# Second layer's experts in whole float32: two products in column halves, eleven more weight places

## The chip, the core and the metric

One Trainium2 chip, one core of it. The metric is the time on the device in microseconds, the median over runs; lower is better. A core has TensorE (PE), VectorE (DVE), ScalarE (ACT), GpSimd (POOL), SyncE (SP, which here only issues transfers) and 16 DMA engines.

## What is computed

Two layers. In each, four token mixers (retention, neighbourhood attention, an S5 scan, windowed attention) work on 512 tokens of width 1024 beside 256 context tokens, and behind them comes a mixture of 32 experts with a two-step router. The second layer runs its experts for the 512 tokens alone. The part that matters here, of the reference:

```python
def hier_moe(xf, rw1, rb1, rw2, rb2, w1, w3, w2):
    ...
    top_v, top_i = lax.top_k(lg2, TOP_K)
    gate = p_grp * jax.nn.softmax(top_v, axis=-1)
    ...
    def expert_block(args):
        xblk, e = args
        hid = jax.nn.silu(xblk @ w1[e]) * (xblk @ w3[e])
        return hid @ w2[e]

    yb = lax.map(expert_block, (xb, blk_expert)).reshape(cap, d)
    y = jax.ops.segment_sum(yb * buf_gate[:, None].astype(yb.dtype), buf_tok, num_segments=n + 1)
```

All is float32. w1 and w3 of an expert are 1024 x 512, w2 is 512 x 1024: three times 2 MB, so 32 experts of a layer read 201 MB.

## The kernel before

*Weights.* A `Stream` (lines 133 to 205) brings weights through fixed places of 512 KB in SBUF, 128 partitions of 2 x 512 float32. `want` (line 156) notes which slice comes next; `load` (line 171) issues a transfer on SP's queue (line 175) whenever a place is free; `feed` (line 178) takes the oldest landed place and splits it into a pair of tiles in the format fp32r, and the place is free again. The split (line 434) is a copy to the high part on ScalarE (line 436) and a subtraction for the low part on VectorE (line 437). There are five pairs, in an arena of their own (`parts`, which the profile calls big_r). `take` hands landed pairs to a product and `release` gives them back.

*A product* (line 553) makes three passes over TensorE for each slice of 128 rows, high by high, high by low and low by high, on lines 560 to 562, into PSUM.

*An expert.* Tokens of an expert are gathered from DRAM by an indirect transfer on GpSimd's queue (line 1894) into 56 rows in the second layer (72 in the first). `turn_x` and `turned` transpose them on TensorE (line 1827), four transposes to a call, and split the result into high and low. `hidden` (line 1839) runs `product` for exp_w1, then for exp_w3, each with eight slices; between the two it transposes the hidden rows of the expert before and the tokens of the next. SiLU is on ScalarE (line 1851), the product of the two halves on VectorE (line 1852). `out_rows` (line 1856) multiplies by exp_w2 on lines 1865 to 1867, 24 passes into two PSUM tiles, and VectorE scales the rows by gate and modulation (line 1874). A scatter that adds (line 1897, GpSimd's queue) puts them into the output rows in DRAM; each waits for the one before.

*Order.* `moe` (line 1890) runs hidden(e), then the output of e-1, for 32 experts; the weights are wanted in the same order, exp_w1 whole, exp_w3 whole, then exp_w2 of the expert before. `moe_open` (line 1876) takes the tiles of the stage and adds places, which come free as the mixers' and the router's tiles end. Before the experts, `moe` feeds four places with GpSimd as the engine of the subtraction (line 1922) and six with VectorE (line 1926), beside the routing. A loop over tokens beyond the 56 rows (line 1977) follows; with this input it runs no turn.

A scheduler of the language settles the order of instructions on each engine from the program and its tiles; the order on SP's queue follows the order of `want`.

## Time and profile before

| What | Value |
|---|---|
| time, median of 3 runs | 2857.58 us (2855.39 to 2862.84) |
| the profiled execution's own time | 2857.83 us |
| its span, first to last instruction | 2856.0 us |
| mean granted TensorE clock | 0.97 |
| busy share of the span: PE, DVE, ACT, POOL | 93%, 73%, 51%, 23% |
| moved by DMA in the whole span | 699.37 MB, 245 GB/s |

The span is cut by the page into 40 slices of 71.4 us. The second layer's experts fill the slices from the 32nd on (2237 us), the first layer's from about the 14th to the 21st. Busy shares are over the whole span, so a stage has to be read by its own stretch. Weights that wait in places, and the places that wait for a split, do not show as busy time anywhere; they show as waits of SP's queue, in front of line 175. The tiles have names: raw and big hold places and other float32 data, big_r the split pairs, sc the PSUM tiles of `hidden`, mm those of `out_rows`, tr those of transposes, mod those of the modulation product (line 482).

### The profile page before, as it was taken

The page shows a single profiled execution, that of the slowest core. Times are in us where ns is not written, and L with a number is a line of the kernel's source. Part 1 is how long each engine was busy: PE and PEld are TensorE (multiplying, and loading weights), DVE is VectorE, ACT ScalarE, POOL GpSimd, SP SyncE. Part 2 cuts the span into 40 slices and gives each one's busy share as a digit, 9 for nine tenths or more (in the row PEclk, how much of TensorE's full clock was granted, in tenths as well). Part 3 has the DMA queues.
Part 4 walks back from the last instruction along what each step waited for, and adds up shares of the span by engine and source line. Part 5 has one row for each costly group of instructions (what it writes and reads, how often), then busy time and mean ns, then how long its engine had stood idle before and what let it go on. Part 6 is the DMA issues. An engine that isn't in the chain of part 4 may idle for free. (4 is left out here: it accounts for less than half of the span.)

```text
span 2856.0 us, 39093 instructions
## 1 busy us (share of the span) xinstructions
PE 2662.6 (93%) x13190; PEld 1808.5 (63%) x13190; DVE 2077.0 (73%) x3921; ACT 1463.3 (51%) x2219; POOL 659.4 (23%) x596
## 2 busy tenths in 40 slices
PE   5999999999998899999996799999999799999997
PEld 2777767777786556665553477777887455555443
DVE  6754455656347989998886668746846999998887
ACT  3322343532232678887775334533324577776665
POOL 2231211011013621111112311021101533323432
PEclk8999999999999899999998999999999799999999
DMA  8687545244427899999997765465435899999994
GB/s 280 198 266 221 153 133 185 81 151 154 159 96 256 287 342 376 359 354 356 372 374 234 230 178 166 125 208 168 137 109 192 275 369 376 372 358 335 343 348 119
DMA packets 268646, 699.37 MB, mean 245 GB/s; under 512 B 64836, under 2 KB 83512, under 8 KB 268440
## 3 DMA queue, kind: packets, MB, share of 16 engines
q1 hardware_dynamic: 170672, 531.30, 51.9%
q0 software_dynamic: 39744, 113.86, 14.9%
q10 hardware_dynamic: 58024, 51.65, 5.8%
q8 instruction: 106, 1.74, 0.2%
q14 instruction: 100, 0.82, 0.1%
HBM read 622.48 MB, written 80.44 MB: 246 GB/s over the span
## 5 line engine op out<-in xcount | busy, mean ns | idle before, releaser
L437 DVE TENSOR_TENSOR big_r<-big,big_r 128x1024 fp32r<-128x1024 f32 x512 | 613.8, 1223 | 80.1 <-ACT big_r L436 76.3
L436 ACT CAST big_r<-big 128x1024 fp32r<-128x1024 f32 x517 | 532.9, 1052 | 146.9 <-PE mm L562 74.9
L560 PE MATMUL mm<-big_r,turned 128*128 128x512 f32 x1248 | 515.7, 414 | 13.4 <-ACT turned L436 7.0
L561 PE MATMUL mm<-big_r,turned 128*128 128x512 f32 x1248 | 506.7, 406 | 3.8 <-DVE big_r L437 3.8
L562 PE MATMUL mm<-big_r,turned 128*128 128x512 f32 x1248 | 506.3, 406 | 0.3 <-DVE turned L437 0.3
L437 DVE TENSOR_TENSOR big_r<-raw,big_r 128x1024 fp32r<-128x1024 f32 x392 | 464.1, 1218 | 41.5 <-ACT big_r L436 35.4
L436 ACT CAST big_r<-raw 128x1024 fp32r<-128x1024 f32 x395 | 403.6, 1051 | 65.8 <-PE sc L562 32.8
L561 PE MATMUL sc<-big_r 128*72 128x512 f32 (+1 forms) x1024 | 409.7, 400 | 19.5 <-DVE big_r L437 18.4
L560 PE MATMUL sc<-big_r 128*72 128x512 f32 (+1 forms) x1024 | 407.3, 398 | 0.0
L562 PE MATMUL sc<-big_r 128*72 128x512 f32 (+1 forms) x1024 | 405.1, 396 | 0.0
L560 PEld LDWEIGHTS mm<-big_r,turned 128*128 128x128 f32 x1248 | 238.3, 191 | 96.2 <-issue 28.7
L562 PEld LDWEIGHTS mm<-big_r,turned 128*128 128x128 f32 x1248 | 238.0, 191 | 57.7 <-issue 6.5
L561 PEld LDWEIGHTS mm<-big_r,turned 128*128 128x128 f32 x1248 | 238.7, 191 | 55.8 <-issue 5.1
L561 PEld LDWEIGHTS sc<-big_r 128*72 128x72 f32 (+1 forms) x1024 | 138.4, 135 | 139.0 <-DVE big_r L437 55.0
L1897 POOL DMA_INDIRECT out_dram<-big x32 | 159.5, 4984 | 264.6 <-DVE big L1874 260.2
L1866 PE MATMUL mm<-big_r 128*72 128x512 f32 (+1 forms) x512 | 204.0, 398 | 0.4
L560 PEld LDWEIGHTS sc<-big_r 128*72 128x72 f32 (+1 forms) x1024 | 139.1, 136 | 100.6 <-ACT big_r L436 7.7
L1867 PE MATMUL mm<-big_r 128*72 128x512 f32 (+1 forms) x512 | 201.3, 393 | 0.0
L562 PEld LDWEIGHTS sc<-big_r 128*72 128x72 f32 (+1 forms) x1024 | 138.8, 136 | 85.9 <-issue 1.2
L1865 PE MATMUL mm<-big_r 128*72 128x512 f32 (+1 forms) x512 | 184.5, 394 | 1.1 <-DVE big L1874 0.6
L1382 ACT ACTIVATE wa<-mm 128x512 f32<-128x512 f32 x80 | 47.7, 596 | 230.2 <-PE mm L562 229.9
L1368 DVE SCALAR_TENSOR_TENSOR wa<-wa,mm 128x512 f32<-128x512 f32 x60 | 41.1, 686 | 138.6 <-PE mm L562 132.6
(381 smaller groups left out, 3764.5 us busy)
## 6 DMA issues: line engine op xcount, KB each, us to landing
big<-in_exp_w_dram SPq DMA_DIRECT2D x393, 512.0 KB
raw<-in_exp_w_dram SPq DMA_DIRECT2D x375, 512.0 KB
big<-in_mod_w_dram SPq DMA_DIRECT2D x96, 512.0 KB
big<-in_w_in_dram SPq DMA_DIRECT2D x68, 512.0 KB
big<-in_w_in_dram SPq DMA_DIRECT2D x48, 256.0 KB
big<-s_wc POOLq DMA_DIRECT2D x16, 576.0 KB, 5.6
big<-s_ph POOLq DMA_DIRECT2D x16, 388.0 KB, 3.9
big<-s_wb POOLq DMA_DIRECT2D x16, 384.0 KB, 4.1
```

The lines of the kernel that those rows point to most:

```text
L436: return (self.nc.scalar.copy(hi, src), (v or self.nc.vector).tensor_tensor(lo, src, hi.bitcast(F32), op=OP.subtract))
L437: (v or self.nc.vector).tensor_tensor(lo, src, hi.bitcast(F32), op=OP.subtract))
L560: nc.tensor.matmul(ps, ah, wh, start=(k == 0), stop=False)
L561: nc.tensor.matmul(ps, ah, wl, start=False, stop=False)
L562: nc.tensor.matmul(ps, al, wh, start=False, stop=(k == n - 1))
L1368: nc.vector.scalar_tensor_tensor(tg, tg, 1.0, pb, op0=OP.add, op1=OP.mult)
L1382: nc.scalar.activation(tg, pg, AF.Tanh, scale=0.5)
L1865: nc.tensor.matmul(o, hh.v[:, k, :n], w[:, 0, half], start=(k == 0), stop=False)
L1866: nc.tensor.matmul(o, hh.v[:, k, :n], w[:, 1, half], start=False, stop=False)
L1867: nc.tensor.matmul(o, hl.v[:, k, :n], w[:, 0, half], start=False, stop=(k == 3))
L1897: scatter = lambda y, i: nc.gpsimd.indirect_dma_start(out=ya, out_offset=bass.IndirectOffsetOnAxis(ap=i, axis=0), in_=y, in_offset=None, b ...
```

## The change

In the second layer the weights are used as they land, in float32, and are not split. `want` marks such a slice as whole, `feed` leaves it alone, and `take_whole` hands the places themselves to the products; a place goes back to the stream when both products of its slice are issued. A float32 product is one instruction for a slice in place of three. `hidden_whole` writes the product with exp_w1 to PSUM partitions 64 to 119 and the one with exp_w3 to partitions 0 to 55 of one tile, slice by slice in turn, and `want_hidden` orders exp_w1 and exp_w3 in turn to suit. `out_whole` does the same with the two column halves of exp_w2. The transposed tokens and hidden rows are copied once (ScalarE or VectorE) in place of a split. The gate is copied to partitions 64 and up, where the second half's rows lie.

`moe_open` gives the arena of the pairs up in the second layer, opens a float32 arena of the same size instead, named whole, and lays eleven places and the transposed tiles into it. These places are added behind all others. The feeds beside the routing fall away in the second layer. The first layer stays as it is.

The diff, without the loop that runs no turn:

```diff
--- before.py
+++ after.py
         for b in stages:
             self.stages.remove(b)
-    def want(self, pieces):
-
-        self.todo.append(pieces)
+    def want(self, pieces, whole=False):
+
+        self.todo.append((pieces, whole))
         self.load()
     def want_cols(self, src, pieces, nk):
...
     def load(self):
         while self.todo and self.stages and not self.pause:
             b = self.stages.pop(0)
-            for dst, src in self.todo.pop(0):
+            pieces, whole = self.todo.pop(0)
+            for dst, src in pieces:
                 self.prog.nc.sync.dma_start(dst(b.v), src)
-            self.staged.append(b)
+            self.staged.append((b, whole))
     def feed(self, v=None):
-        if self.staged and self.pairs:
-            b, s = self.staged.pop(0), self.pairs.pop(0)
+        if self.staged and self.pairs and not self.staged[0][1]:
+            b, s = self.staged.pop(0)[0], self.pairs.pop(0)
             with self.prog.after(*self.behind):
                 self.prog.split(s.v[:, 0], s.v[:, 1], b.v, v)
             self.ready.append(s)
-            if b in self.once:
-                self.once.remove(b)
-            else:
-                self.stages.append(b)
-            self.load()
+            self.back(b)
             return True
+
+    def back(self, b):
+
+        if b in self.once:
+            self.once.remove(b)
+        else:
+            self.stages.append(b)
+        self.load()
+
+    def take_whole(self, n):
+
+        out, self.staged = self.staged[:n], self.staged[n:]
+        assert len(out) == n and all(w for _, w in out) and not (self.ready or self.live)
+        return [b for b, _ in out]
+
     def take(self, n):
...
         bigs = pool("bigs", 1)
         n_r, n = 13312, 18784
-        self.parts = Arena(bigs.tile([128, n_r], F32R, name="big_r"), n_r)
+        self.parts_pool = tc.alloc_tile_pool(name="parts", bufs=1, side="left")
+        ctx.callback(lambda: self.parts_pool.release())
+        self.parts = Arena(self.parts_pool.tile([128, n_r], F32R, name="big_r"), n_r)
         self.arena = Arena(bigs.tile([128, n], F32, name="big"), n)
...
+
+    def open_whole(self):
+
+        self.parts_pool.release()
+        self.parts_pool = self.tc.alloc_tile_pool(name="whole", bufs=1, side="left")
+        n = 13312
+        self.parts = Arena(self.parts_pool.tile([128, n], F32, name="whole"), n)
+        self.s.pairs = []
     def rbuf(self, *shape):
...
     def want_hidden(self, s, l, e):
-        for name in ("exp_w1", "exp_w3"):
-            src = self.rows_at(name, l, e).rearrange("(p k) c -> p k c", k=8)
+        srcs = [self.rows_at(name, l, e).rearrange("(p k) c -> p k c", k=8) for name in ("exp_w1", "exp_w3")]
+        if l:
             for k in range(0, 8, 2):
-                s.want([(lambda st: st, src[:, k : k + 2])])
+                for src in srcs:
+                    s.want([(lambda st: st, src[:, k : k + 2])], True)
+        else:
+            for src in srcs:
+                for k in range(0, 8, 2):
+                    s.want([(lambda st: st, src[:, k : k + 2])])
     def want_out(self, s, l, e):
         src = self.rows_at("exp_w2", l, e).rearrange("(p k) c -> p k c", k=4)
         for k in range(4):
-            s.want([(lambda st: st.rearrange("p h c -> p (h c)"), src[:, k])])
+            s.want([(lambda st: st.rearrange("p h c -> p (h c)"), src[:, k])], bool(l))
     def rows_at(self, name, l, e):
         w = self.A[name]
...
-        self.split(hi.v[:, ks, :n], lo.v[:, ks, :n], tr[:, :, :n])
+        if lo is None:
+            (nc.vector.tensor_copy if q else nc.scalar.copy)(hi.v[:, ks, :n], tr[:, :, :n])
+        else:
+            self.split(hi.v[:, ks, :n], lo.v[:, ks, :n], tr[:, :, :n])
     def turn_x(self, n, x, b=None):
...
         nc.vector.tensor_tensor(hid[:n].rearrange("p (k c) -> p c k", k=4), t.rearrange("p (c k) -> p c k", k=4),
                                 hp[1][:n].rearrange("p (c k) -> p c k", k=4), op=OP.mult)
         return hid
+
+    def hidden_whole(self, n, xT, between):
+
+
+        nc = self.nc
+        x = xT[0].v
+        two = n <= 64
+        ps = [self.ps_sc.tile([128, 512], F32, name="sc") for _ in range(1 if two else 2)]
+
+        o = [ps[0][64 : 64 + n], ps[0][:n]] if two else [ps[0][:n], ps[1][:n]]
+        for j in range(4):
+            ws = self.s.take_whole(2)
+            for k in (2 * j, 2 * j + 1):
+                for m in range(2):
+                    nc.tensor.matmul(o[m], x[:, k, :n], ws[m].v[:, k % 2], start=(k == 0), stop=(k == 7))
+            for w in ws:
+                self.s.back(w)
+            if j == 1:
+                between()
+        hid = self.hid.v
+        t = self.wa()[:n]
+        nc.scalar.activation(t, o[0], AF.Silu)
+        nc.vector.tensor_tensor(hid[:n].rearrange("p (k c) -> p c k", k=4), t.rearrange("p (c k) -> p c k", k=4),
+                                o[1].rearrange("p (c k) -> p c k", k=4), op=OP.mult)
+        return hid
+
+    def out_whole(self, n, y, hT, gate, by):
+
+        nc = self.nc
+        h = hT[0].v
+        two = n <= 64
+        ws = self.s.take_whole(4)
+        ps = [self.ps_mm.tile([128, 512], F32, name="mm") for _ in range(1 if two else 2)]
+        at = [0, 64 if two else 0]
+        o = [ps[0][:n], ps[-1][at[1] : at[1] + n]]
+        for k, w in enumerate(ws):
+            for half in range(2):
+                nc.tensor.matmul(o[half], h[:, k, :n], w.v[:, half], start=(k == 0), stop=(k == 3))
+            self.s.back(w)
+        for half in range(2):
+            c = slice(half * 512, half * 512 + 512)
+            nc.vector.scalar_tensor_tensor(y[:n, c], o[half], gate(at[half]), by[at[half] : at[half] + n, c],
+                                           op0=OP.mult, op1=OP.mult)
+        self.copied = None
     def out_rows(self, n, y, hT, gate, by):
...
                 nc.vector.scalar_tensor_tensor(y[:n, c], ps[half][:n], gate, by[:n, c], op0=OP.mult, op1=OP.mult)
     def moe_open(self, l, C):
-        self.xT = [(self.rbuf(128, 8, C), self.rbuf(128, 8, C)) for _ in range(2)]
-        self.hT = self.rbuf(128, 4, C), self.rbuf(128, 4, C)
+        if l:
+            self.open_whole()
+
+            room = self.rbuf(128, 12, 128)
+            extra = [self.rbuf(128, 2, 512) for _ in range(11)]
+            room.free()
+            self.xT = [(self.rbuf(128, 8, C), None) for _ in range(2)]
+            self.hT = self.rbuf(128, 4, C), None
+        else:
+            self.xT = [(self.rbuf(128, 8, C), self.rbuf(128, 8, C)) for _ in range(2)]
+            self.hT = self.rbuf(128, 4, C), self.rbuf(128, 4, C)
         self.xs0 = self.buf_old(128, D)
         self.nc.gpsimd.memset(self.xs0.v, 0.0)
         self.more = more = [self.buf(128, 2, 512) for _ in range(8 - l)]
...
+        if l:
+            self.s.add(extra, [])
         self.i_x = 0
     def moe(self, l, tiles, C, f_d, h_d, idx, x1, rest):
...
-            self.out_rows(C, y, hT, gate[:C, e : e + 1], by)
+            if l:
+                self.out_whole(C, y, hT, lambda p: gate[p : p + C, e : e + 1], by)
+            else:
+                self.out_rows(C, y, hT, gate[:C, e : e + 1], by)
+            assert ys[e % 2] not in [b for b, _ in self.s.staged]
             scatter(y[:C], idx[:C, 1, e : e + 1].bitcast(I32))
         get(0)
...
                 nc.gpsimd.memset(b.v[:1, 0, :1], 0.0)
         self.s.add(later, [])
         self.s.hold = False
-        for _ in range(4):
-            self.s.feed(nc.gpsimd)
+        if not l:
+            for _ in range(4):
+                self.s.feed(nc.gpsimd)
         with self.after(self.routed):
-            for _ in range(6):
-                self.s.feed()
+            if not l:
+                for _ in range(6):
+                    self.s.feed()
             put_gates, blocks, scatters = rest()
         x1.v = x1.v.rearrange("p (k c) -> p k c", k=2)
         self.more.append(x1)
         self.s.add([x1], [])
         gate = self.gate
+        if l:
+
+            nc.scalar.copy(gate[64 : 64 + C], gate[:C])
         self.hid = self.buf(128, 512)
         ys = self.ys
         xT = self.turn_x(C, xs[0].v)
...
-            h = self.hidden(C, xT, between)
+            h = (self.hidden_whole if l else self.hidden)(C, xT, between)
```

The order of instructions moves at two places that matter here. The first is SP's queue where the second layer's experts begin, behind the last loads of the mixers' weights (in_w_out_dram). Before:

```order
L175 DMA raw<-in_exp_w_dram 128x1024 x10
L175 DMA big<-in_exp_w_dram 128x1024
L175 DMA raw<-in_exp_w_dram 128x1024 x2
L175 DMA big<-in_exp_w_dram 128x1024 x11
L175 DMA raw<-in_exp_w_dram 128x1024 x9
```

and now:

```order
L176 DMA raw<-in_exp_w_dram 128x1024 x8
L176 DMA big<-in_exp_w_dram 128x1024
L176 DMA whole<-in_exp_w_dram 128x1024 x3
L176 DMA big<-in_exp_w_dram 128x1024
L176 DMA whole<-in_exp_w_dram 128x1024
L176 DMA big<-in_exp_w_dram 128x1024
L176 DMA whole<-in_exp_w_dram 128x1024 x7
```

The eleven places (whole) come in between the last free places of the mixers (big), three, one and seven in a row; before, each of these loads went to a place that a split or another tile's end had to free.

The second is TensorE inside one of the second layer's experts, the end of `hidden` and the beginning of the output. Before:

```order
L560 MATMUL sc<-big_r 56x512
L561 MATMUL sc<-big_r 56x512
L562 MATMUL sc<-big_r 56x512
L1865 MATMUL mm<-big_r 56x512
L1866 MATMUL mm<-big_r 56x512
L1867 MATMUL mm<-big_r 56x512
```

and now, with the transposes that stand in the middle of `hidden_whole`:

```order
L1854 MATMUL tr<-cst,big 128x56 x8
L1899 MATMUL sc<-raw,whole 56x512 x2
L1854 MATMUL tr<-cst,big 128x56 x4
L1899 MATMUL sc<-raw,whole 56x512 x6
L1922 MATMUL mm<-raw,whole 56x512 x2
```

Three instructions for a slice and a column half have become one, and the eight of a group alternate between the two halves; between them still stand the transposes, eight for the next tokens and four for the hidden rows.

## Rows read from the trace of the kernel before

**Rows 1.** Page, part 2: DMA share in tenths and GB/s, 40 slices of 71.4 us.
```profile
DMA  8687545244427899999997765465435899999994
GB/s 280 198 266 221 153 133 185 81 151 154 159 96 256 287 342 376 359 354 356 372 374 234 230 178 166 125 208 168 137 109 192 275 369 376 372 358 335 343 348 119
```

**Rows 2.** Table by stretch, the second layer's experts; its first line names the columns.
```profile
core 0: us, PE busy (x) PEld busy (x) DVE busy (x) ACT busy (x) POOL busy (x), PEclk, DMA share, GB/s
2300.00:2540.00 240.00, 240.00 (x1131) 133.34 (x1129) 228.81 (x243) 186.67 (x217) 85.68 (x28) 1.00 1.02 374
2540.00:2808.00 268.00, 256.42 (x1169) 134.78 (x1168) 236.09 (x250) 179.85 (x222) 92.20 (x26) 1.00 0.97 340
2808.00:2856.00 48.00, 32.27 (x139) 16.57 (x137) 30.56 (x31) 19.67 (x23) 9.43 (x3) 0.90 0.15 20
2237.00:2310.00 73.00, 67.36 (x335) 38.26 (x335) 67.12 (x121) 50.75 (x66) 44.58 (x22) 0.92 0.91 319
```

**Rows 3.** Groups of instructions by line and form, from 2200 us to the end.
```profile
L437 DVE TENSOR_TENSOR big_r<-big,big_r 128x1024 fp32r<-128x1024 f32 x190 | 225.7, 1215 | 20.8 <-ACT big_r L436 19.9
...
L560 PE MATMUL sc<-big_r 128*56 128x512 f32 x512 | 203.2, 397 | 0.0
...
L1827 PE MATMUL tr<-cst,big 56*128 56x56 f32 x384 | 37.7, 232 | 0.1
```

**Rows 4.** Waits of SP's queue: 2200 to 2856 us, then 1200 to 1300 (total, times, longest).
```profile
SPq L175 <- DVE big_r L437: 415.2, 348, 4.2
...
SPq L175 <- DMA raw<-in_exp_w_dram: 39.8, 33, 2.9
SPq L175 <- DMA big<-in_exp_w_dram: 33.2, 27, 2.3
```

**Rows 5.** Timeline of TensorE: the float32 modulation product at 15.5, 25.8 and 272.0 us.
```profile
15.51 1.92 PE L482 MATMUL mod<-big,scT 128*32 128x512 f32 x4 [2.14 <-DMA big<-in_mod_w_dram]
...
25.82 1.05 PE L482 MATMUL mod<-big,scT 128*32 128x512 f32 x4 [0.24 <-DMA big<-in_mod_w_dram]
...
272.00 1.06 PE L482 MATMUL mod<-big,scT 128*32 128x512 f32 x8
```

**Rows 6.** DMA view, 2237 us to the end: all packets of that stretch.
```profile
DMA packets 57393, 201.30 MB, mean 325 GB/s; under 512 B 8344, under 2 KB 8352, under 8 KB 57344
```

**Rows 7.** Table by stretch, columns as in rows 2: first layer's experts, then the beginning.
```profile
1200.00:1300.00 100.00, 100.00 (x483) 62.19 (x482) 91.38 (x91) 84.65 (x105) 19.96 (x12) 1.00 1.03 360
1450.00:1510.00 60.00, 58.23 (x270) 34.27 (x269) 51.95 (x53) 42.87 (x55) 6.22 (x4) 1.00 1.03 386
12.00:15.50 3.50, 1.05 (x4) 0.14 (x4) 0.00 (x0) 0.71 (x3) 0.00 (x0) 0.74 1.03 402
15.50:24.00 8.50, 6.44 (x14) 0.75 (x16) 5.56 (x45) 4.91 (x14) 0.59 (x1) 0.51 1.04 348
24.00:37.00 13.00, 10.00 (x40) 1.30 (x36) 10.47 (x87) 1.91 (x8) 2.09 (x4) 1.00 1.04 377
```

**Rows 8.** Timeline of GpSimd, then VectorE, in the second layer's routing.
```profile
2211.73 8.01 POOL L437 TENSOR_TENSOR big_r<-raw,big_r 128x1024 fp32r<-128x1024 f32 x3 [0.79 <-ACT big_r L436]
...
2214.62 2.90 DVE L1549 TENSOR_TENSOR wa<-big 128x512 f32<-128x512 f32 x1
...
2217.52 2.24 DVE L1554 TENSOR_TENSOR ss<-ss_all 128x1 f32<-128x1 f32 x1
...
2220.12 2.20 DVE L1637 TENSOR_SCALAR big<-cst,big 128x4 f32<-128x4 f32 x1
...
2227.43 0.68 DVE L1549 TENSOR_TENSOR wa<-big 128x512 f32<-128x512 f32 x1
```

**Rows 9.** Timeline of the end: TensorE's and VectorE's last work, GpSimd's last scatter.
```profile
2841.47 0.40 PE L1867 MATMUL mm<-big_r 128*56 128x512 f32 x1
...
2841.21 1.44 DVE L1874 SCALAR_TENSOR_TENSOR big<-mm,gate,big 56x512 f32<-56x512 f32 x2 [1.30 <-PE mm L1867]
...
2844.10 1.44 POOL L1897 DMA_INDIRECT out_dram<-big  x1 [4.02 <-issue]
```

## What the change should do to the time

> **What bounds the kernel now.** I start with the page's slices, because the change touches only the last fifth of the program. [rows 1] In slices 32 to 39 of 40 the DMA digit is 9 and the transfer rate lies between 335 and 376 GB/s, so the second layer's experts stream weights about as fast as anything in this program does. The first question is therefore what paces that stream: the memory side, or the engines that free the places into which the weights land.
>
> The table by stretch answers it in two halves. [rows 2] From 2300 to 2540 us TensorE is busy 240.00 of 240 us, VectorE 228.81, and the transfers fill a DMA share of 1.02 at 374 GB/s: everything is full at once. From 2540 to 2808 TensorE is at 256.42 of 268 and the DMA share is 0.97 at 340 GB/s. [rows 3] The big costs are the splits: VectorE's subtraction on line 437 takes 1215 ns for one place, 190 of them from this group of places alone, and the three passes of lines 560 to 562 follow it. [rows 4] The queue that issues the loads, SP, waits for that subtraction 348 times, 415.2 us in all, over the second layer's end. So a load is not issued when the memory is ready; it is issued when VectorE has split a place. TensorE, VectorE and the transfers are within a few per cent of one another, with the place as the coupling.
>
> After the last weights the picture differs. [rows 2] In 2808 to 2856 the DMA share is 0.15 while TensorE still works 32.27 us. These 48 us are split, product and scatter of the experts whose weights were already there, and no transfer overlaps them.
>
> **The change, part by part.** All of it lies behind the routing of the second layer; what runs before is in the same order on every engine.
>
> *Products.* An expert now has 72 passes of 512 columns and 12 transposes. [rows 2] TensorE runs 1131 instructions in 240 us, 0.212 us apart, so 84 take 17.8 us. After the change there are 24 float32 products, in 12 pairs that write different column halves, and the same 12 transposes. The trace has this form elsewhere: the modulation product of line 482 runs float32 products of 512 columns side by side, two records for each. [rows 5] At 25.82 us two such products (x4 records) take 1.05 us; at 272.00 four of them (x8) take 1.06. Four cost what two cost, so products in different columns do overlap, and I take 1.05 us for a pair: 12 x 1.05 = 12.6 us. The transposes are 384 for 37.7 us [rows 3], 1.2 us for an expert. TensorE then needs 13.8 us for an expert instead of 17.8.
>
> *Splits.* ScalarE's and VectorE's passes over the weights go away; of VectorE's work an expert keeps one product, one copy and two scalings. No engine but TensorE stands between landing and release of a place: SP's loads wait for PE and for earlier loads alone.
>
> *Transfers.* Bytes stay the same. [rows 6] From 2237 us to the end 201.30 MB move, 32 experts with their gathers and scatters, 6.3 MB each. At 374 GB/s that is 16.8 us for an expert, above TensorE's 13.8 us. So the transfers become the bound, with 11 more places to ride out a short stall, and the question is at what rate they run when nothing else holds them.
>
> *The rate.* No stretch of this stage is free of places, so I bound it by neighbours. [rows 7] The first layer's experts wait for their own transfers: between 1200 and 1300 us SP waits 39.8 and 33.2 us for weight transfers [rows 4], so nothing else paces them. There the rate is 360 GB/s at a share of 1.03, with gathers of 72 rows instead of 56, and 386 later on. A short stretch with almost nothing else running shows 402. The second layer's own fullest stretch, 374 at share 1.02 [rows 2], is the nearest in kind (same gathers, same scatters) and lies in the middle; I take it, and keep 360 to 402.
>
> The Trainium skill, "DMA: Bandwidth & Descriptors" (Where 436 GB/s comes from), says that a transfer from HBM to SBUF is bound by the HBM side at about 358 GB/s. By that rule the estimate for the sum below is 2811. The rows above disagree: 374 over 240 us and 386 over 60 us.
>
> *Start.* [rows 8] GpSimd split four places in the routing (three of them 8.01 us), and VectorE's small steps beside it ran long: line 1549 took 2.90 us against 0.68 us later, and lines 1554 and 1637 took 2.24 and 2.20 us on one and four columns. These splits are gone; if each of the three steps had lost the 2.2 us of line 1549, routing and first gather come some 6 us earlier (bounds: nothing and 7), and I use 5. I let the stream be full from 2232 us instead of reaching a share of 0.91 from 2237 to 2310 [rows 2]: SP finds seven fresh places in a row behind the two that it had, 4.7 MB, enough until TensorE frees others. The two halves' outputs and the gate copied to partition 64 cost one ScalarE copy of a few columns, hidden in the first gather's flight.
>
> *End.* Today the last weights land at about 2808 and the span ends at 2856. [rows 9] The last scaling takes 1.44 us for its two halves, the last scatter starts at 2844.10, and the span ends 11.9 us later. After the change what follows the last landing is one pair (1.05), two scalings (1.44), the wait for the scatter before it (under 1 us; the two are five transfers apart) and the same 11.9 us: 15 us instead of 48.
>
> *Sum.* 201.30 MB at 374 GB/s is 538 us; 2232 + 538 = 2770 for the last landing, 38 us before today's; + 15 = 2785 for the span, against 2856.0. The profiled execution's time is 1.83 us above its span, which gives **2787 us**. That execution, 2857.83, stands 0.25 us above the median of the runs, so nothing is corrected for it. Of the 71 us, 38 come from the stream and 33 from the end.
>
> The clock is the condition for 13.8 us. [rows 7] TensorE waited for transfers like this from 24 to 37 us, busy 10.00 of 13, at a granted clock of 1.00 (2.4 GHz), and from 15.5 to 24 us it was busy 6.44 of 8.5 at 0.51 (1.2 GHz), right after a stretch in which it had worked 1.05 of 3.5 us. At 13.8 of 16.8 us it is nearer to the former. At the lower level a pair takes 1.92 us for the x4 of [rows 5]; then TensorE would be busy all the time, which is the state in which it has clock 1.00 in [rows 2]. A brief fall is covered by some 35 places, nearly three experts.
>
> **The rivals.**
>
> *The transfers are slower than I take them.* The 340 GB/s of 2540 to 2808 came at a share of 0.97, so the packets themselves took longer there than in 2300 to 2540 (350 GB/s for a share of 1 against 367). If the memory side does that and not the places, the rate is about 360, as in the first layer. Starting at 2237: 201.30 / 0.360 = 559, + 2237 + 15 + 1.8 = 2813. With 340 throughout it is 592 and 2846, a gain of 0.4% that comes from the end alone. For it: the first layer shows 360 with its own transfers as the wait. Against it: SP's wait on the splits, and 386 in the same first layer.
>
> *The transfers are faster.* With no splits reading and writing the same memory, 402 may hold: 501 + 2232 + 16.8 = 2750. Against it: the 402 comes from 3.5 us without scatters. The Trainium skill, "HBM Reference" (Specifications), says that a core streaming alone measures about 425 GB/s; by that the estimate is 2723. No stretch quoted here reaches it with gathers and scatters beside it.
>
> *The pairs do not overlap, and TensorE is the bound: slower than before.* The products alternate between the halves and read different weights from different places, and between them stand full-width transposes. If each product ran alone, at 0.96 us (half of 1.92, the group at half clock), an expert would take 24 x 0.96 + 1.2 = 24.2 us. From the first product at about 2239 (2246 now) that is 2239 + 774 + 17 = 3030 us. The point at which it decides is a pair of 1.40 us: there TensorE needs 18 us, today's time. For it: pairs of 64 columns with 512 columns of float32 are not in the trace. Against it: x8 in 1.06 us.
>
> *The change does not do what it says*, for instance since a place is released late and the loads still queue behind one another. A place goes back when both products of its slice are done, and the last slice of an expert waits longest; then the end is still shorter by 33 us, and the time about 2825, just above the range.
>
> **How the numbers follow.** Forecast (rate 367 to 386, 2768 to 2797): 0.60. Slower transfers, 2798 to 2846, the release rival included: 0.25, of which 0.07 lies above 2815. Faster transfers: 0.09. Pairs serial or the clock low: 0.05. Rest, near no change: 0.01. The range from 2752 to 2815 leaves out the serial case (0.05), no change (0.01), the slowest transfers (0.07) and the fastest ones (0.03), 0.16 in all. A measurement of this kernel tells 0.3%, some 8.6 us, from no change. Faster by more than that: 0.60 + 0.24 + 0.09 = 0.93; the same 0.02; slower 0.05.
>
> **What would show it.** Right: in the stretch 2300 to 2540 the DMA share stays at 1.02 or above while TensorE falls to some 80% and VectorE under 30%; SP waits for its own transfers and hardly for PE; the SiLU of successive experts are 16.8 us apart; between the last weight transfer and the end lie 15 us. Wrong: TensorE at 100% with a pair above 1.4 us or a granted clock near 0.5; SP waiting for PE while the DMA share is under 1; or a rate of 360 GB/s and less at full share.

## The result, and the profile after

The changed kernel takes 2769.84 us (median of 4 runs, 2766.78 to 2772.12) against 2856.48 beside it: a ratio of 0.9694, 95% interval 0.9682 to 0.9705, 86.6 us less. The forecast was 2787, with 2752 to 2815 as its range. The profiled execution took 2768.99 us, its span is 2767.0.

The page's slices, now of 69.2 us each, first the DMA share in tenths, then GB/s:

```profile
DMA  8686545343535799999999766546542699999997
GB/s 277 204 266 206 177 134 182 117 138 112 185 125 188 261 319 376 373 356 351 365 366 342 247 199 169 161 125 206 172 141 89 209 375 384 389 383 384 383 382 288
```

Seven slices of the last stage stand between 375 and 389 GB/s, where [rows 1] had 335 to 376. The table by stretch (its columns are those of [rows 2]):

```profile
2230.00:2300.00 70.00, 62.82 (x314) 22.03 (x314) 20.07 (x48) 7.97 (x19) 18.82 (x18) 0.89 1.03 392
2300.00:2540.00 240.00, 221.26 (x892) 64.19 (x890) 42.51 (x58) 19.15 (x46) 36.92 (x30) 1.00 1.03 384
2540.00:2750.00 210.00, 190.99 (x724) 52.06 (x720) 36.31 (x49) 15.33 (x36) 27.02 (x22) 1.00 1.02 380
2750.00:2767.00 17.00, 2.40 (x10) 0.37 (x8) 1.50 (x2) 0.00 (x0) 2.47 (x2) 0.73 0.21 30
```

The DMA share is at 1.02 or 1.03 from 2230 us to the last landing at about 2751, at 392, 384 and 380 GB/s. VectorE's busy time in 2300 to 2540 fell from 228.81 us to 42.51. What SP's queue waits for in 2300 to 2540 (total, times, longest) has turned over with it:

```profile
SPq L176 <- DMA big<-in_exp_w_dram: 61.5, 56, 2.4
SPq L176 <- DMA raw<-in_exp_w_dram: 59.6, 59, 2.1
SPq L176 <- DMA whole<-in_exp_w_dram: 53.1, 47, 2.3
SPq L176 <- PE mm L1922: 7.4, 25, 0.4
```

174 us go to earlier loads, 7.4 and a few more to TensorE, none to VectorE, which was the first of these waits before [rows 4]. The SiLU of the 32 experts:

```profile
L1906 ACT ACTIVATE wa<-sc x32: 593/593/594, 2245.5 to 2743.5; 56x512 f32<-56x512 f32 x32
```

In that line's starts the first distances are 14.2 and then six of 11.6 to 12.7 us, while TensorE works off what had landed before; from the ninth distance on they are 17.4 us on average, the pace of the transfers. The pace of TensorE alone can be read at the second expert's weights:

```profile
2241.76 3.65 PE L1899 MATMUL sc<-big,whole 128*56 128x512 f32 x16
...
2245.54 3.65 PE L1899 MATMUL sc<-raw,whole 128*56 128x512 f32 x16
```

Sixteen records are eight products, four pairs, begun within 3.57 us (2241.76 to 2245.33, where the next instruction starts): 0.89 us for a pair. And the end, on TensorE, VectorE and GpSimd:

```profile
2751.69 1.07 PE L1922 MATMUL mm<-big,whole 128*56 128x512 f32 x4 [0.17 <-SPq L2072]
...
2752.81 1.53 DVE L1926 SCALAR_TENSOR_TENSOR big<-mm,gate,big 56x512 f32<-56x512 f32 x2 [3.51 <-PE mm L1922]
...
2755.17 1.44 POOL L1982 DMA_INDIRECT out_dram<-big  x1 [4.14 <-DVEq L2072]
```

From the last pair to the end of the span it is 15.3 us, where it had been 48 behind the last landing [rows 2, 9]. Of the 89 us between the two spans some 56 lie before the last landing (about 2808 before, about 2751 now) and 33 behind it.

### The profile page after: what moved, and what is told of

It reads as the page before. It is cut to its first block, busy times and chain, and to the rows that moved or that the text cites. A ratio compares the mean times of both kernels' runs of the same rounds, so it can differ in the third digit from the quotient of the medians.

```text
span 2767.0 us, 36035 instructions
## 1 busy us (share of the span) xinstructions
PE 2542.8 (92%) x12422; PEld 1628.8 (59%) x12422; DVE 1619.0 (59%) x3477; ACT 1071.9 (39%) x1804; POOL 511.0 (18%) x592
## 3 DMA queue, kind: packets, MB, share of 16 engines
q0 software_dynamic: 39744, 113.86, 15.3%
## 5 line engine op out<-in xcount | busy, mean ns | idle before, releaser
L459 DVE TENSOR_TENSOR big_r<-big,big_r 128x1024 fp32r<-128x1024 f32 x322 | 387.8, 1225 | 58.1 <-ACT big_r L458 53.2
L458 ACT CAST big_r<-big 128x1024 fp32r<-128x1024 f32 x326 | 337.8, 1055 | 111.2 <-PE mm L584 74.8
L459 DVE TENSOR_TENSOR big_r<-raw,big_r 128x1024 fp32r<-128x1024 f32 x202 | 241.2, 1219 | 30.5 <-ACT big_r L458 27.6
L458 ACT CAST big_r<-raw 128x1024 fp32r<-128x1024 f32 x202 | 207.0, 1048 | 36.1 <-PE sc L584 14.7
L583 PE MATMUL sc<-big_r 128*72 128x512 f32 x512 | 205.8, 402 | 6.9 <-DVE big_r L459 6.4
L582 PE MATMUL sc<-big_r 128*72 128x512 f32 x512 | 204.0, 399 | 0.0
L584 PE MATMUL sc<-big_r 128*72 128x512 f32 x512 | 202.7, 396 | 0.0
L1979 POOL DMA_INDIRECT big<-f_d,big x64 | 78.9, 1232 | 425.9 <-PE tr L1854 405.7
L1899 PE MATMUL sc<-big,whole 128*56 128x512 f32 x332 | 123.8, 606 | 17.6 <-DMA big<-in_exp_w_dram 17.1
L1899 PE MATMUL sc<-raw,whole 128*56 128x512 f32 x376 | 128.5, 627 | 6.5 <-DMA raw<-in_exp_w_dram 6.1
L1982 POOL DMA_INDIRECT ya<-big x32 | 54.1, 1692 | 341.6 <-ACT big L1946 312.8
L1899 PE MATMUL sc<-whole 128*56 128x512 f32 x316 | 105.2, 605 | 11.4 <-DMA whole<-in_exp_w_dram 11.2
```

What stands on the lines that cost most here:

```text
L458: return (self.nc.scalar.copy(hi, src), (v or self.nc.vector).tensor_tensor(lo, src, hi.bitcast(F32), op=OP.subtract))
L459: (v or self.nc.vector).tensor_tensor(lo, src, hi.bitcast(F32), op=OP.subtract))
L582: nc.tensor.matmul(ps, ah, wh, start=(k == 0), stop=False)
L583: nc.tensor.matmul(ps, ah, wl, start=False, stop=False)
L584: nc.tensor.matmul(ps, al, wh, start=False, stop=(k == n - 1))
L1899: nc.tensor.matmul(o[m], x[:, k, :n], ws[m].v[:, k % 2], start=(k == 0), stop=(k == 7))
```

## The experiments

The theory that I tested: the transfers are the bound from the stage's start to the last landing; all else is hidden. Times are medians; ratios are against the kernel before the change, run beside each.

### Without the eleven extra places

```diff
-            extra = [self.rbuf(128, 2, 512) for _ in range(11)]
+            extra = []
```

> The changed kernel without the eleven extra places (24 places in the cycle, as before the change). Theory 'the transfers are the bound from the start of the stage to the last landing': the places matter only before the first product, when TensorE frees nothing; eleven loads of 1.37 us come up to 15 us later, then the stream is full again at 380 GB/s and more with the DMA share at 1.02 or above. Time 2777 to 2787, experts still 17.3 us apart from the eighth on. Rival 'the places carry the stream all the way': SP waits for TensorE throughout, share under 1, experts over 18 us apart, 2795 or more. Rival 'the places are worth nothing': 2770.

2773.87 us, ratio 0.9703 (0.9686 to 0.9719).

```profile
2300.00:2540.00 240.00, 219.57 (x844) 60.60 (x840) 41.05 (x56) 17.97 (x42) 34.71 (x28) 1.00 1.03 386
```

The stream is as full with 24 places, 386 GB/s, and the experts are 17.4 us apart from the eighth on. The difference of 4 us is less than the 7 to 17 that I expected, and the two intervals can't tell it from nothing. TensorE gives places back fast enough.

### Products one by one

```diff
-        two = n <= 64
+        two = False
...
-        two = n <= 64
+        two = False
```

> The changed kernel with its products one by one: both products of a slice write PSUM partitions 0 to 55 of two tiles instead of the two column halves. Theory 'a pair costs 0.91 us because its two products overlap': a product alone costs the same 0.91 us, an expert 24 x 0.91 + 1.2 = 23 us of TensorE, which then is the bound; 2236 + 32 x 23 + 17 = 2990 us, some 135 us slower than before the change. Rival 'the two products of a pair follow one another and each takes 0.46 us': nothing changes, 2770.

2952.78 us, ratio 1.0331 (1.0293 to 1.0368); 21.9 us from expert to expert. TensorE's timeline, and the first wait of SP's queue from 2300 to 2700:

```profile
2500.87 3.60 PE L1899 MATMUL sc<-big,whole 128*56 128x512 f32 x8
...
2504.30 3.60 PE L1899 MATMUL sc<-raw,whole 128*56 128x512 f32 x8
```

```profile
SPq L176 <- PE sc L1899: 211.1, 144, 3.5
```

Eight records, now four products, take 3.43 us: 0.86 us for one, about what a pair takes (0.86 to 0.89). So the two halves overlap almost wholly, and without that the change loses some 94 us against the kernel before. The time is below the 2990 that I expected because I had taken 0.91 for one product. The mechanism of my third rival is real; it did not occur.

### Half the bytes, before and after

In both kernels each load brings half of its slice from the fifth (sixth) expert on; half of each place keeps old data. The edit in the kernel before (the other is the same, with `e > 4`):

```diff
-                s.want([(lambda st: st, src[:, k : k + 2])])
+                if l and isinstance(e, int) and e > 3:
+                    s.want([(lambda st: st[:, :1], src[:, k : k + 1])])
+                else:
+                    s.want([(lambda st: st, src[:, k : k + 2])])
...
-            s.want([(lambda st: st.rearrange("p h c -> p (h c)"), src[:, k])])
+            if l and isinstance(e, int) and e > 3:
+                s.want([(lambda st: st[:, 0], src[:, k, :512])])
+            else:
+                s.want([(lambda st: st.rearrange("p h c -> p (h c)"), src[:, k])])
```

> The kernel before the change, but from the fifth expert of the second layer on each weight transfer brings only half of its slice (256 KB; the other half of the place keeps old data, so the output is not the computation's). Theory 'before, the engines paced the stage and the transfers only kept up': with half the bytes the experts stay 17.5 us or more apart in the first half of the stage, and the second half, 19.4 us apart, gains at most to 17.9: 2820 to 2857. Rival 'the transfers were a bound of their own': the experts come 16.5 us apart or closer throughout, under 2805.

> The changed kernel with half the bytes in the same way, from the sixth expert on. Theory 'the transfers are the bound now, with TensorE's 11.6 us an expert next': the experts stay 11.6 us apart to the end, as the first seven are now; 2245 + 31 x 11.7 + 25 = 2633 us, some 137 us under the changed kernel. Rival 'something else, the chain of an expert or the gathers and scatters, holds them at 15 us or more': 2735 or more.

The kernel before: 2836.24 us, and the table by stretch:

```profile
2300.00:2540.00 240.00, 240.00 (x1126) 133.28 (x1125) 228.43 (x243) 186.00 (x214) 82.65 (x28) 1.00 0.68 197
2540.00:2700.00 160.00, 160.00 (x752) 88.81 (x751) 151.99 (x162) 124.27 (x143) 52.39 (x18) 1.00 0.68 197
```

With a DMA share of 0.68 TensorE is at 100% in both halves and the experts are 17.9 us apart throughout. In the first half nothing changed, so the transfers did not pace it. That TensorE did, and not VectorE with its 228.43 us, I read from the waits from 2300 to 2540: TensorE waits for nothing, while ScalarE's copies, with which a split begins, wait for TensorE to give pairs back:

```profile
ACT big_r L436 <- PE sc L562: 29.0, 85, 0.6
```

No run takes work from VectorE alone, so this part is argued. The second half, 19.4 us apart with TensorE at 96% and 340 GB/s [rows 2], came down to 17.9: there the transfers took part, although SP's queue named VectorE. What made them slower there stays open.

The changed kernel: 2626.92 us, 11.6 us from expert to expert.

```profile
2300.00:2540.00 240.00, 240.00 (x1242) 82.52 (x1240) 60.94 (x83) 24.45 (x62) 50.79 (x41) 1.00 0.97 307
```

So 143 us lie between the changed kernel and its next bound, TensorE. That shows the transfers as the bound most directly.

### Other engines' traffic

```diff
+            self.passes(2, 2 if j < 2 else 1)
...
+
+    def passes(self, na, nv):
+        src, hi, lo = (b.v for b in self.idle)
+        for _ in range(na):
+            self.nc.scalar.copy(hi, src)
+        for _ in range(nv):
+            self.nc.vector.tensor_tensor(lo, src, src, op=OP.subtract)
...
+            self.passes(1, 1)
...
+            self.idle = [extra.pop() for _ in range(3)]
+            for b in self.idle:
+                self.nc.vector.memset(b.v, 0.0)
```

> The changed kernel with idle passes added: for each of the second layer's experts 12 copies of 128x1024 on ScalarE and 10 subtractions on VectorE, over three of the extra places (so eight extra places are left), with no tie to the weights. They load the two engines nearly as the splits did. Theory 'the stream ran at 340 to 374 GB/s before because loads waited for places, not because the engines use the same memory': the stretch 2300 to 2540 stays at 380 GB/s or more, time 2768 to 2778. Rival 'the splits' traffic slowed the packets': the rate falls to 374 or under at a share of 1.02, 2785 or more.

2830.91 us, ratio 0.9895 (0.9870 to 0.9920), a time in the rival's range, but not by way of the rate:

```profile
2220.00:2300.00 80.00, 30.63 (x173) 14.19 (x173) 75.25 (x162) 70.86 (x85) 18.82 (x19) 0.62 0.64 230
2300.00:2540.00 240.00, 186.65 (x848) 62.24 (x844) 224.92 (x210) 222.28 (x243) 48.23 (x28) 0.89 1.03 386
2420.00:2460.00 40.00, 24.46 (x104) 8.21 (x102) 36.17 (x34) 34.36 (x38) 6.01 (x4) 0.79 1.03 392
2540.00:2700.00 160.00, 113.67 (x466) 37.09 (x464) 146.11 (x134) 132.35 (x143) 24.80 (x16) 0.78 0.90 315
```

From 2300 to 2540 ScalarE and VectorE are busy 222.28 and 224.92 of 240 us, and the transfers still move 386 GB/s at a share of 1.03. The rival, packets slowed by the splits' traffic, falls for a stream that is full. What was lost came another way, in two places: 12 and 11 MB less than in the changed kernel. At the start, passes stand between the small steps of the routing: the first gather begins at 2258.03 instead of 2227.12, and from 2220 to 2300 the transfers move 230 GB/s, where the changed kernel has 381. Later the scheduler put the passes in bunches, and the product on line 1908 stood behind eleven of them; TensorE's largest wait from 2450 to 2700, and the first wait of SP's queue from 2540 to 2700:

```profile
PE tr L1854 <- DVE big L1908: 80.5, 12, 8.0
SPq L176 <- PE mm L1930: 57.9, 22, 7.3
```

TensorE, busy 24.46 of 40 us from 2420, is at a granted clock of 0.79 there. From 2540 it frees places too late: SP waits for it 105 of 160 us in all, and the share is 0.90.

### Splits on GpSimd beside the routing

```diff
-        for _ in range(4):
-            self.s.feed(nc.gpsimd)
+        if not l:
+            for _ in range(4):
+                self.s.feed(nc.gpsimd)
```

> The kernel before the change without the four splits on GpSimd in the second layer's routing (the weights are split later, by VectorE). Theory 'these splits slow the routing by 5 us': the first product of the experts starts 4 to 7 us earlier against the routing's start, but VectorE has four splits of 1.2 us more afterwards, in a stage where it is nearly full: 2851 to 2858 in all. Rival 'the routing is not held up by them': the first product starts at the same distance, time unchanged or up to 6 us longer.

2866.36 us, ratio 1.0029 (1.0017 to 1.0040): slower by 7 us. VectorE, GpSimd, the router's first product and TensorE's waits from 2240 to 2320, and then the first gather before the change:

```profile
2217.61 0.69 DVE L1549 TENSOR_TENSOR wa<-big 128x512 f32<-128x512 f32 x1
```

```profile
2238.80 5.26 POOL L1894 DMA_INDIRECT big<-f_d,big  x1 [3.08 <-DVE big L1682]
```

```profile
L1509 PE MATMUL sc<-big,wa x64: 194/279/429, 2174.4 to 2230.8; 128*128 128x36 f32 x64
```

```profile
PE tr L1827 <- DMA big<-f_d,big: 13.5, 2, 8.8
```

```profile
2241.08 1.08 POOL L1894 DMA_INDIRECT big<-f_d,big  x1 [3.37 <-DVE big L1693]
```

Line 1549 takes 0.69 us, not the 2.90 of [rows 8], so the splits did slow the routing. From the router's first product to the first gather it is 64.4 us (2174.4 to 2238.80), where it was 69.9 before the change (2171.2 to 2241.08): 5.5 us less, near the 5 of my term. Here the gain is lost again, and the time lies above what the theory and its rival had: the gather itself lasts 5.26 us against 1.08, TensorE waits 13.5 us for tokens, and VectorE has four more splits (the third and fourth distance of experts are 22.5 and 20.8 us, 18.0 and 17.9 before). In the changed kernel the first gather starts at 2227.12, 14 us earlier than before it and 63.9 us behind the router's first product: these 6 us and the 8 of the next run.

### The arena of the pairs in a pool of its own

```diff
-        self.parts = Arena(bigs.tile([128, n_r], F32R, name="big_r"), n_r)
+        self.parts_pool = tc.alloc_tile_pool(name="parts", bufs=1, side="left")
+        ctx.callback(lambda: self.parts_pool.release())
+        self.parts = Arena(self.parts_pool.tile([128, n_r], F32R, name="big_r"), n_r)
```

> The kernel before the change with one part of it alone: the arena of the split pairs in a pool of its own on the left side; nothing else moves. The changed kernel ran 8.3 us ahead at its 10400th TensorE instruction (2202 us), before anything of the change is executed but this. Theory 'the layout in memory makes the earlier stages faster': 2848 to 2852, and the same lead at that instruction. Rival 'the lead is the difference from one execution to another': 2853 to 2862 and no steady lead.

2849.69 us (10 runs) against 2859.16 (18 runs), ratio 0.9974 (0.9962 to 0.9987): 4 to 11 us, from the place of one arena. The router's product of the second layer (first and last start at the end of the row), before, in this run, and in the changed kernel:

```profile
L1509 PE MATMUL sc<-big,wa x64: 193/279/429, 2171.2 to 2232.9; 128*128 128x36 f32 x64
```

```profile
L1511 PE MATMUL sc<-big,wa x64: 193/279/429, 2163.4 to 2224.7; 128*128 128x36 f32 x64
```

```profile
L1531 PE MATMUL sc<-big,wa x64: 193/279/429, 2163.2 to 2218.7; 128*128 128x36 f32 x64
```

Both stand 8 us ahead before anything else of the change is executed. One execution alone would not show it: in the kernel before with half the bytes this product begins at 2167.3, in the one-by-one run, which has the new place, at 2170.7. The medians of the 10 and 18 runs do. The order of instructions on the engines is the same as before. Why the place matters I did not find out.

### What the gathers and scatters cost the stream

Five runs ask what holds the transfers at 384 GB/s. Empty rows skipped in the scatter:

```diff
-            bounds_check=T * 128 + 127, oob_is_err=True, compute_op=OP.add)
+            bounds_check=T * 128 - 1, oob_is_err=False, compute_op=OP.add)
```

> The changed kernel with the scatter's bound set so that the empty rows of an expert (slots without a token) are skipped instead of being added to spare rows. Counting by the capacity, 56 rows for 32 used on average in the second layer and 72 for 48 in the first, some 24 of each scatter's rows go. Theory 'the transfers are the bound, so bytes that go shorten it': the scatters' share of the DMA time falls from about 0.06 to 0.035 in both layers' experts, 8 to 14 us in each: 2742 to 2760. Rival 'scatters fit in beside the weights at no cost': 2770.

2769.59 us, ratio 0.9688 (0.9668 to 0.9708): no change, so my theory missed. DMA queues in 2300 to 2540 (packets, MB, share), the changed kernel and then this one:

```profile
q1 hardware_dynamic: 23752, 86.49, 92.6%
q0 software_dynamic: 2400, 5.47, 9.9%
```

```profile
q1 hardware_dynamic: 23699, 86.29, 94.6%
q0 software_dynamic: 2400, 3.95, 6.8%
```

The bytes of the scatter went, the 2400 packets of GpSimd's queue did not, and the weights (q1) got nothing of it. Hence the next two. A second queue for the weights:

```diff
+    two, odd = False, False
+
...
-                self.prog.nc.sync.dma_start(dst(b.v), src)
+                q = self.prog.nc.scalar if self.two and self.odd else self.prog.nc.sync
+                q.dma_start(dst(b.v), src)
+            self.odd = not self.odd
...
+            self.s.two = True
```

> The changed kernel with every second weight load of the second layer's experts issued on ScalarE's queue instead of SP's. Skipping the scatter's empty rows took 1.5 MB off the stretch 2300 to 2540 and left the weights at 360 GB/s (86.49 and 86.29 MB in 240 us), so what binds is not the sum of all packets. Theory 'the memory side gives the weights about 360 GB/s': a second queue changes nothing, 2766 to 2775 (some us more if ScalarE's SiLU stands behind an issue). Rival 'one queue's stream is at its own limit': with two the weights' rate rises to 375 GB/s or more and the time falls to 2745 or under.

2786.56 us, ratio 0.9749 (0.9731 to 0.9766). The stretch 2300 to 2540 and TensorE's wait in it:

```profile
2300.00:2540.00 240.00, 199.68 (x840) 64.72 (x838) 41.12 (x56) 16.63 (x42) 34.90 (x28) 0.82 1.03 388
```

```profile
PE tr L1858 <- ACT whole L1861: 40.3, 14, 5.6
```

388 GB/s against 384: a second queue brings next to nothing, and the next run has 409 with one. The kernel is 17 us slower all the same, above both times that I expected. TensorE waits 40.3 us for ScalarE's copies, which now stand behind loads that wait, and falls behind a stream that itself ends earlier, at about 2745 us instead of 2751. So it still works for 24 us when the last weights have landed, and the end takes 39 us where the changed kernel has 16:

```profile
2745.00:2769.00 24.00, 23.41 (x118) 7.74 (x116) 5.59 (x8) 2.47 (x6) 3.14 (x3) 1.00 0.17 24
```

And the weights without gathers and scatters:

```diff
-            scatter(y[:C], idx[:C, 1, e : e + 1].bitcast(I32))
+            if not l or e < 4 or e > 29:
+                scatter(y[:C], idx[:C, 1, e : e + 1].bitcast(I32))
...
-            if e + 2 < NEXP:
+            if e + 2 < NEXP and not (l and e > 3):
```

> The changed kernel without the gathers of tokens from the seventh expert on and without the scatters of the fifth to thirtieth expert in the second layer (those rows of the output are left out, later experts work on old tokens). Theory 'the weights have a bound of their own near 360 GB/s, and gathers and scatters pass beside them': the weights' rate in 2300 to 2540 stays within 355 to 368 GB/s, experts 17.0 us apart or more, 2755 to 2772. Rival 'packets of all queues share one bound, 384 GB/s in all': the weights take over the whole of it, 16.4 us apart, 2735 to 2745.

2710.94 us, ratio 0.9481 (0.9461 to 0.9502), 15.5 us on average from expert to expert (9th to 30th distance, as for the 17.4):

```profile
2300.00:2540.00 240.00, 230.08 (x980) 70.13 (x978) 47.49 (x66) 20.83 (x49) 0.00 (x0) 1.00 1.03 409
```

409 GB/s, nearly all of it weights: no bound of 360, and my theory falls again; so does the rival, which gave the weights 384. 59 us of the changed kernel are what 26 gathers and 26 scatters take from the stream, although both together move only 5.47 of 92.13 MB in 2300 to 2540. Without the scatters alone:

```diff
-            scatter(y[:C], idx[:C, 1, e : e + 1].bitcast(I32))
+            if not l or e < 4 or e > 29:
+                scatter(y[:C], idx[:C, 1, e : e + 1].bitcast(I32))
```

> The changed kernel without the scatters of the fifth to thirtieth expert in the second layer, with all gathers (the output lacks those experts). Without gathers and scatters the weights ran at 409 GB/s, 15.35 us an expert, against 17.3 with both. Theory 'the scatter, which reads and adds what it writes, costs most of the 1.9 us': experts 15.4 to 15.9 us apart, 2711 to 2730. Rival 'gather and scatter cost by their rows': 56 of some 88 rows go, about two thirds, 16.0 us apart, 2730 to 2738. Rival 'the gather costs it': 16.8 us or more, 2752 and over.

2738.51 us, ratio 0.9588 (0.9566 to 0.9610), 16.1 us apart, 397 GB/s. Of the 1.9 us that an expert loses (17.4 to 15.5), the scatter takes 1.3 and the gather, by subtraction, 0.6: about as the 56 rows of a scatter to the 32 that a gather fills on average, the second of the three that I had. Last, fewer rows:

```diff
-    def __init__(self, ctx, tc, A, out, cap=(72, 56)):
+    def __init__(self, ctx, tc, A, out, cap=(72, 48)):
```

> The changed kernel with room for 48 rows of an expert in the second layer instead of 56 (with these inputs no expert has more than 47, so the loop over tokens beyond it still runs no turn). Theory 'the scatters' rows cost the stream': 8 of 56 rows go, a seventh of at most 1.9 us an expert, 0.27 x 32 = up to 9 us: 2761 to 2768. Rival 'the number of empty rows does not matter, as when they were skipped': 2769 to 2772.

2759.09 us, ratio 0.9663 (0.9644 to 0.9683), 17.0 us apart:

```profile
2300.00:2540.00 240.00, 223.71 (x881) 59.84 (x878) 43.51 (x60) 17.91 (x44) 34.86 (x30) 1.00 1.03 391
```

```profile
q0 software_dynamic: 1908, 4.93, 8.8%
```

Here GpSimd's packets fall from 2400 to 1908 and 11 us go, 2 more than I allowed at most. The two intervals just meet, but the experts, 17.0 us apart against 17.4, say the same. Skipping cut bytes and gained nothing, this cuts rows and gains: the cost seems to go with the rows, or the packets, that an indirect transfer is given. That is not shown for good: only 56 and 48 rows were run, and 48 rows divide evenly among the 16 DMA engines where 56 do not. How a row holds up the weights stays open. This kernel beats both; its capacity fits these inputs (no expert beyond 47 rows) and leaves more to the loop for others.

## Why the prediction was right, and by how much its terms were off

*The bound.* Right. The transfers set the pace, SP waits for them, TensorE has slack, and with half the bytes of the weights 143 us go.

*The rate.* Right in kind and 2.7% low: 374 taken, 384 and 380 measured. Against the profiled execution the forecast was 18 us high (2787 and 2768.99), and 12 of these are the rate: at the 383 GB/s that moved from 2230 us to the last landing, 201.30 MB take 526 us, not 538. The range's bounds held. That 374 came so near is in part luck. What I took for the pace of the transfers before was that of an engine, most likely TensorE, in the first half (half the bytes left it at 17.9 us), so 374 was what the engine asked for, not what the transfers could do; and what they can do depends on the gathers and scatters, which the sum had only as bytes.

The first rival, slower packets in the second half, falls: 380 GB/s there now. Its reading, 350 GB/s for a share of 1 as slower packets, was not sound either: the run with idle passes shows the same 350 (315 at 0.90), and there SP waits for TensorE. The second rival's 402 is passed only without gathers and scatters. The Trainium skill's 358 GB/s for the HBM side ("DMA: Bandwidth & Descriptors", Where 436 GB/s comes from) is passed, with one core at work, by 384 with everything and by 409 with weights nearly alone. The 425 GB/s that the Trainium skill's "HBM Reference" (Specifications) gives for a core alone is nearer to the latter, and no run reached it.

*Distance of experts.* I wrote 16.8 us by dividing what was left at 2237 among 32 experts, though two experts' weights had landed by then. An expert moves 12 x 0.524 = 6.29 MB of weights and 0.4 MB beside them (5.47 MB in 240 us); 6.69 MB at 384 GB/s is 17.4 us, as measured. The sum goes by all bytes and did not suffer.

*Start.* The routing's 6 us are there, but some 8 us more (4 to 11 by the medians) came from the arena's place, which no term had. At 2230 us 199.89 MB were still to move, where my sum had 201.30 at 2232: 1.4 MB and 2 us, some 6 us together, nearly all of the rest of the difference. The eleven places, which I counted on at the start, made a difference of 4 us, not clear of noise.

*TensorE.* A pair is 0.86 to 0.89 us, not 1.05: the row that I took held one lone group, and the last pair of the stage, alone too, shows 1.07. So an expert takes 11.6 us, not 13.8. It lies beside the transfers and cost the sum nothing. That TensorE would show 80% busy was wrong: it shows 92%, though 11.6 of 17.4 us would make 67%; busy time is no measure of its slack here. The clock condition held, 1.00 at 221.26 of 240 us.

*End.* 15 us foretold, 15.3 measured.

## What to carry to other kernels

When the busy shares of three engines lie within a few per cent, halve the bytes or the work of one of them in an experiment: one run says whether that one paces the stage, where a queue's waits name only the last link. A float32 product that fits half the columns is worth laying beside another: here one pair replaced six passes and took ScalarE and VectorE out of the weights' path. And once the transfers are the bound, look at the small ones: here 6% of the bytes cost 11% of the stream.

## What the runs showed of the hardware

A float32 product of 512 columns took 0.86 us, and two in different column halves took 0.86 to 0.89 us together. Weights in packets of 4 KB ran at 409 GB/s over 240 us when nothing was gathered or scattered. The place of an arena in SBUF changed the time of earlier stages by 4 to 11 us with the same order of instructions. While GpSimd split weights, a step of VectorE took 2.90 us in place of 0.69. And GpSimd's own time for a scatter fell with the change; before it and after it, over the second layer:

```profile
L1897 POOL DMA_INDIRECT out_dram<-big x32 | 159.5, 4984 | 264.6 <-DVE big L1874 260.2 <-issue 4.3
```

```profile
L1982 POOL DMA_INDIRECT out_dram<-big x32 | 46.5, 1454 | 127.6 <-DVE big L1926 123.1 <-DVEq L2072 4.1 <-issue 0.3
```

4984 ns against 1454 for one. VectorE's busy time alone does not explain it. The first layer's scatters before the change, of 72 rows, with VectorE busy 91.38 of 100 us [rows 7], and those of the second layer in the run with idle passes, with VectorE busy 224.92 of 240:

```profile
L1897 POOL DMA_INDIRECT ya<-big x32: 1486/1726/1764, 1002.9 to 1538.4; - x32
L1994 POOL DMA_INDIRECT out_dram<-big x32 | 63.1, 1972 | 116.9 <-DVE big L1935 111.6 <-DVEq L2084 4.1 <-DVE whole L1857 0.9
```

1726 ns at the median and 1972 on average. What made the 4984 stays open.
